# Residual two-block transformer on one core: 512-column products from a joined high and low operand, the last residual by transposes, squares on ScalarE, and SyncE outside the branch

## The chip, the cores and the metric

One Trainium2 chip, one core of it. The metric is the device time of one launch in microseconds (us). The kernel before was run three times; its median is 1277.7 us (1276.87 to 1277.78). PE is TensorE, ACT is ScalarE, DVE is VectorE, POOL is GpSimd, SP is SyncE, whose queue issues the transfers from HBM.

## The reference, cut to what matters

256 tokens of width 1024 go through two models in a row, all in float32.

- Block 1: an input projection into two attentions (8 heads each) and two gates, `mixed = sigmoid(gate_a)*(o_a@w_o_mla) + sigmoid(gate_b)*(o_b@w_o_moba)`, `x += mixed@w_out`, then a mixture of 32 experts (each token uses 2) and a final norm.
- Block 2, layer 0: `x += even_mixer(norm(x))` (a gated convolution beside differential attention). Layer 1: `x += odd_mixer(norm(x))` (stick-breaking attention, 16 heads of 64).
- In both layers of block 2 then: `x += mem_attention(norm(x), memory)` (4 heads of 256) and `x += ffn(norm(x))` with `u = causal_conv3(h@w_up)`, `gate, val = split(u)`, `(silu(gate)*val)@w_down`, where `w_up` is 1024 x 5632 and `w_down` 2816 x 1024.

All weights are read once; most of the time is their products with 256 token columns.

## The kernel before, in words

**Products.** A float32 product is made from three float32r products: the weight and the activation are each split into a high and a low part, and `h*xh + h*xl + l*xh` is summed in PSUM (`mm3`). An activation lies feature-major as `[128, 8 chunks, 256 tokens]` in two tiles, `xh` and `xl` (`xtiles`, `parts`). A weight comes in slabs of 1 MB (`slab`): SP issues the transfer into `w`, then in two halves ACT copies `w` to `h` and DVE subtracts `w - h` into `l`. `w`, `h` and `l` have three buffers each.

**fm** multiplies a slab of 8 chunks x 256 output columns: for each chunk and each of the two blocks of 128 output columns three matmuls of 256 moving columns, 48 in a slab, all into one PSUM bank (tag `g`, three banks), the two blocks side by side. The evictions read this bank with one DVE instruction, a multiplication by the row of `1/rms` (`rbc`):

```
b = self.fm(self.slab(a[f"w_up{l}"][i], 256), x)
nc.vector.tensor_tensor(u[:, :, 2:], self.two(b), self.rep(rbc), ALU.mult)
```

**Where the change touches it.** `block1_attention` makes the gates (8 slabs); `mem_attention` the queries (4 slabs in each layer, `head_norm` evicts them); `odd_mixer` queries and keys (8 slabs); `ffn` the up-projection (22 slabs in each layer, pairs of gate and value columns). After two up slabs, `ffn` does one slab of the down-projection (`down`), whose four PSUM banks (two of tag `a`, two of tag `b`) stay open for the whole stage. In layer 0, `down` makes 48 matmuls of 256 columns a slab, in layer 1 (token-major, for the output) 24 of 512. In layer 1 the residual enters these four banks first, by 16 products of `self.x` with the identity; at the end ACT and DVE in turn copy the banks to `o`, and SP stores them.

**rsq** makes `1/sqrt` by ACT (Ln, Exp) and one Newton step on DVE, whose first instruction is `u*u`. `transposed` turns a tile of probabilities with PE and copies it from PSUM with DVE.

**Order of the work.** `Recorder` records every operation, then `plan` puts them in order by a list schedule with a cost for each (a 256-column float32r matmul at 109.7 ns, a 512-column one at 216.3 ns), a lag of 200 ns between engines and a number of buffers for each tag; every engine runs its own list in that order. Transfers are issued by SP in the order of recording, each when the plan has a buffer for it. All recorded operations show as line 470.

**The branch.** After the second of eight groups of experts, `moe_late` handles tokens over an expert's 32 slots (none in this run): `values_load` reads a flag into a register of each engine (line 1210), and `tc.If(late > 0)` (line 1220) is taken by all engines, SP too, since the transfers of the branch body are SP's. `plan` lets all engines but SP stop there.

## Time and profile before

| what | value |
|---|---|
| median of 3 runs | 1277.7 us |
| the profiled execution's own time | 1279.2 us |
| its span | 1277.4 us |
| busy: PE, DVE, ACT, POOL | 1224.6, 862.5, 647.3, 7.8 us |
| granted PE clock, mean over the span | 0.977 of full |
| read from HBM | 270.96 MB |

The span is the time from the first to the last instruction in the trace. The profiled execution took 1.8 us more than its span and 1.5 us more than the median. A matmul's duration in the trace overlaps the next one's; how long a stream of matmuls takes is read from their starts, or from the chain of waits, which gives a group's time without overlap.

### The profile page before, as it was taken

The page shows a single profiled execution, that of the slowest core. Times are in us where ns is not written, and L with a number is a line of the kernel's source. Part 1 is how long each engine was busy: PE and PEld are TensorE (multiplying, and loading weights), DVE is VectorE, ACT ScalarE, POOL GpSimd, SP SyncE. Part 2 cuts the span into 40 slices and gives each one's busy share as a digit, 9 for nine tenths or more (in the row PEclk, how much of TensorE's full clock was granted, in tenths as well). Part 3 has the DMA queues.
Part 4 walks back from the last instruction along what each step waited for, and adds up shares of the span by engine and source line. Part 5 has one row for each costly group of instructions (what it writes and reads, how often), then busy time and mean ns, then how long its engine had stood idle before and what let it go on. Part 6 is the DMA issues. An engine that isn't in the chain of part 4 may idle for free.

```text
span 1277.4 us, 22372 instructions
## 1 busy us (share of the span) xinstructions
PE 1224.6 (96%) x9175; PEld 1077.6 (84%) x9175; DVE 862.5 (68%) x1546; ACT 647.3 (51%) x1095; POOL 7.8 (1%) x70
## 2 busy tenths in 40 slices
PE   9999999997889878998999999999999999999998
PEld 8988999664555644897999999999989999999997
DVE  7667677424462345997877977777755587877775
ACT  7655554223242234564545655555766655555543
POOL 0000000000000000000000000000000000000000
PEclk9999999998899989998999999999999999999999
DMA  7623565898999987532441554555433252554541
GB/s 263 245 99 133 207 253 200 335 403 359 419 412 419 416 366 296 198 132 100 162 169 65 200 195 171 195 186 178 165 133 133 93 178 98 193 193 173 184 176 66
DMA packets 40140, 273.51 MB, mean 214 GB/s; under 512 B 4576, under 2 KB 4576, under 8 KB 8032
## 3 DMA queue, kind: packets, MB, share of 16 engines
q1 hardware_dynamic: 40032, 272.03, 56.9%
q8 instruction: 73, 1.20, 0.4%
q14 instruction: 35, 0.29, 0.1%
HBM read 270.96 MB, written 1.05 MB: 213 GB/s over the span
## 4 chain that ended last, share of the span: by engine, by line
PE 90%; DVE 5%; ACT 3%; issue 1%; DMA 1%; SPq 0%; DVEq 0%; ACTq 0%
PE fm L470 51%; PE dn L470 10%; PE tm L470 6%; PE tw L470 4%; PE gu L470 4%; PE by L470 2%; PE oz L470 2%; PE bo L470 1%; DVE l L470 1%; PE sc L470 1%; PE mo L470 1%; PE ga L470 1%; PE ms L470 1%; PE co L470 1%; PE hn L470 1%; ACT h L470 1%
## 5 line engine op out<-in xcount | busy, mean ns | idle before, releaser
L470 PE MATMUL fm<-xh,h 128*128 128x256 f32 x1824 | 529.1, 291 | 7.3 <-ACT h L470 5.0
L470 PE MATMUL fm<-xh,l 128*128 128x256 f32 x1824 | 521.5, 286 | 5.8 <-DVE l L470 5.8
L470 PE MATMUL fm<-xl,h 128*128 128x256 f32 x1824 | 521.0, 286 | 0.0
L470 DVE TENSOR_TENSOR l<-w,h 128x1024 fp32r<-128x1024 f32 (+2 forms) x328 | 383.4, 1190 | 61.7 <-ACT h L470 60.4
L470 ACT ACTIVATE h<-w 128x1024 fp32r<-128x1024 f32 (+2 forms) x328 | 325.6, 1026 | 170.9 <-issue 87.7
L470 PEld LDWEIGHTS fm<-xh,h 128*128 128x128 f32 x1824 | 353.3, 194 | 18.3 <-ACT h L470 7.5
L470 PEld LDWEIGHTS fm<-xh,l 128*128 128x128 f32 x1824 | 353.2, 194 | 8.9 <-DVE l L470 8.6
L470 PEld LDWEIGHTS fm<-xl,h 128*128 128x128 f32 x1824 | 353.6, 194 | 6.5 <-issue 5.1
L470 DVE SCALAR_TENSOR_TENSOR fc<-fu,partile,fc 128x256 f32<-128x256 f32 x176 | 73.4, 478 | 1.3 <-ACT fc L470 1.3
L470 PE MATMUL gu<-w,xs 128*32 128x512 f32 x512 | 69.0, 646 | 0.2 <-PEq L1220 0.2
L470 PE MATMUL dn<-fa,h 128*128 128x256 f32 x352 | 64.2, 282 | 1.1 <-ACT fa L470 0.6
L470 PE MATMUL tm<-l,xh 128*128 128x256 f32 (+2 forms) x204 | 60.1, 296 | 2.7 <-DVE l L470 2.7
L470 PE MATMUL tm<-h,xh 128*128 128x256 f32 (+2 forms) x204 | 61.0, 300 | 0.8 <-DVE x L470 0.6
L470 PE MATMUL tm<-h,xl 128*128 128x256 f32 (+2 forms) x204 | 59.7, 294 | 0.0
L470 PE MATMUL dn<-h,fa 128*128 128x512 f32 x176 | 57.0, 396 | 0.0
L470 DVE TENSOR_TENSOR fu<-fm,rbc 128x512 f32<-128x512 f32 x44 | 30.2, 687 | 38.3 <-PE fm L470 38.0
L470 PEld LDWEIGHTS dn<-fa,h 128*128 128x128 f32 x352 | 54.4, 189 | 1.6 <-ACT fa L470 0.8
L470 DVE SCALAR_TENSOR_TENSOR yl<-by,rw,yh 128x512 fp32r<-128x512 f32 x16 | 12.0, 749 | 57.1 <-ACT yh L470 57.1
L470 PE MATMUL dn<-fa,l 128*128 128x256 f32 x176 | 49.6, 282 | 0.0
L470 ACT ACTIVATE fc<-fc 128x256 f32<-128x256 f32 x44 | 18.4, 418 | 56.3 <-DVE fc L470 56.2
L470 PEld LDWEIGHTS tm<-h,xh 128*128 128x128 f32 x204 | 39.7, 195 | 5.9 <-issue 3.1
L470 ACT ACTIVATE hn_sq<-hn_raw 128x512 f32<-128x512 f32 x20 | 12.3, 624 | 60.7 <-DVE hn_raw L470 60.7
(285 smaller groups left out, 1572.0 us busy)
## 6 DMA issues: line engine op xcount, KB each, us to landing
w<-w_gu SPq DMA_DIRECT2D x64, 1024.0 KB, 9.7
w<-w_up SPq DMA_DIRECT2D x44, 1024.0 KB, 4.9
w<-w_dn SPq DMA_DIRECT2D x32, 1024.0 KB, 11.6
w<-w_down SPq DMA_DIRECT2D x22, 1024.0 KB, 4.9
w<-w_xkv SPq DMA_DIRECT2D x16, 1024.0 KB, 7.7
w<-w_in_d SPq DMA_DIRECT2D x8, 1024.0 KB, 4.8
w<-w_xq SPq DMA_DIRECT2D x8, 1024.0 KB, 4.9
w<-w_xo SPq DMA_DIRECT2D x8, 1024.0 KB, 5.0
```

What stands on the lines that cost most here:

```text
L470: self.last[engine.engine] = getattr(engine, method)(*map(r, a), **{n: r(v) for n, v in k.items()})
```

## The change

- `xtiles` gives one tile `xx` with `xh` and `xl` behind each other (two buffers), in place of two tiles.
- `fm_wide` takes the place of `fm` in the gates (8 slabs), the queries of `mem_attention` but the first of each layer (6), the odd mixer's queries and keys (8) and the up slabs 3 to 19 of each `ffn` (34). For each block of 128 output columns it uses a bank of its own: a matmul of `h` over the 512 columns `xh | xl`, then one of `l` over the 256 columns of `xh` into the first half. ACT copies the first half out, DVE adds the second, and DVE multiplies by `rbc`.
- From block 2 on (`by_act`), the `u*u` in `rsq` is a Square on ACT. In the even mixer the copy of transposed probabilities is ACT's.
- In the last `ffn` the identity products are gone. After the sixth up slab, 16 transposes of `x` go through bank `m` (one buffer) to a tile `xt`, copied by ACT in four pieces. At the end DVE adds `xt` to each of the four banks.
- The flag is loaded by PE, ACT, DVE and POOL alone, the hints ahead of the branch go to these four, and the transfers inside the branch body are POOL's.

```diff
@@ -24,6 +24,7 @@
...
 NPAIR = 22
+NARROW = 3
 WARM = 44
@@ -168,6 +169,7 @@
...
     AHEAD = 120
+    HERE = (mybir.EngineType.PE, mybir.EngineType.Activation, mybir.EngineType.DVE, mybir.EngineType.Pool)
     FIRST = "natural_log_exp_and_others"
@@ -450,7 +452,7 @@
...
             if n in early:
-                for engine in mybir.ALL_ENGINES:
+                for engine in self.HERE:
                     if engine in self.last:
@@ -590,7 +592,8 @@
...
     def xtiles(self):
-        return [self.rec.tile([128, KC, T], F32R, n, n, 2) for n in ("xh", "xl")]
+        both = self.rec.tile([128, 2, KC, T], F32R, "xx", "xx", 2)
+        return both[:, 0], both[:, 1], both
@@ -621,7 +624,10 @@
...
         nc.scalar.activation(u, u, AF.Exp, scale=-0.5)
-        nc.vector.tensor_tensor(t, u, u, ALU.mult)
+        if self.by_act:
+            nc.scalar.activation(t, u, AF.Square)
+        else:
+            nc.vector.tensor_tensor(t, u, u, ALU.mult)
         nc.vector.scalar_tensor_tensor(t, ms, eps, t, ALU.add, ALU.mult)
@@ -689,10 +695,29 @@
...
+    def fm_wide(self, w, x, kcs=None, cols=0):
+
+
+        (h, l), _ = w
+        xh, _, both = x
+        kcs = kcs or [(k, k) for k in range(KC)]
+        bs = []
+        for j in range(2):
+            b = self.bank("g", "fw")
+            s = slice(cols + 128 * j, cols + 128 * j + 128)
+            for i, (k, c) in enumerate(kcs):
+                self.rec.record("tensor", [
+                    ("matmul", (b[:, :512].rearrange("p (a b) -> p a b", a=2), h[:, k, s], both[:, :, c, :]),
+                     dict(start=i == 0, stop=False, skip_group_check=True)),
+                    ("matmul", (b[:, :T], l[:, k, s], xh[:, c, :]),
+                     dict(start=False, stop=i == len(kcs) - 1, skip_group_check=True))])
+            bs.append(b)
+        return bs
+
     def tm(self, b, w, x, kcs, t, cols, first=True, last=True):
@@ -773,12 +798,15 @@
...
-    def transposed(self, p, e):
+    def transposed(self, p, e, by_act=False):
         b = self.bank(p, "pt")
...
         pt = self.temp(p, "pt", [128, 384])
-        self.rec.vector.tensor_copy(pt, b[:, :384])
+        if by_act:
+            self.rec.scalar.activation(pt, b[:, :384], AF.Copy)
+        else:
+            self.rec.vector.tensor_copy(pt, b[:, :384])
         return pt
@@ -929,8 +957,11 @@
...
             for s in range(4):
-                b = self.fm(self.slab(a["w_in_d"][4 * n + s], 256), x)
-                nc.vector.tensor_tensor(gates[n][:, 2 * s:2 * s + 2, :], self.two(b), self.rep(rbc), ALU.mult)
+                for j, b in enumerate(self.fm_wide(self.slab(a["w_in_d"][4 * n + s], 256), x)):
+                    gv = gates[n][:, 2 * s + j, :]
+                    nc.scalar.activation(gv, b[:, :T], AF.Copy)
+                    nc.vector.tensor_tensor(gv, gv, b[:, T:], ALU.add)
+                    nc.vector.tensor_tensor(gv, gv, rbc, ALU.mult)
         for g in gates:
@@ -1207,14 +1238,15 @@
...
         x, hh, hl, rtm, wlate, ident = (v.real() for v in (self.x, hh, hl, rtm, wlate, self.ident))
-        late = nc.values_load(flag.real()[0:1, 0:1], min_val=0, max_val=2 * T)
+
+        late = nc.values_load(flag.real()[0:1, 0:1], engines=rec.HERE, min_val=0, max_val=2 * T)
         tile = lambda shape, name, tag: rec.pools["sb"].tile(shape, F32, name=name, tag=tag, bufs=rec.bufs[tag])
...
             w = tile([128, 512], "wl", "tb")
-            nc.sync.dma_start(w, ap)
+            nc.gpsimd.dma_start(w, ap)
             return w
@@ -1314,7 +1346,13 @@
...
         raw = self.temp(p, "hn_raw", [128, 2, T])
-        nc.vector.tensor_tensor(raw, self.two(b), self.rep(rbc), ALU.mult)
+        if isinstance(b, list):
+            for j in range(2):
+                nc.scalar.activation(raw[:, j, :], b[j][:, :T], AF.Copy)
+                nc.vector.tensor_tensor(raw[:, j, :], raw[:, j, :], b[j][:, T:], ALU.add)
+            nc.vector.tensor_tensor(raw, raw, self.rep(rbc), ALU.mult)
+        else:
+            nc.vector.tensor_tensor(raw, self.two(b), self.rep(rbc), ALU.mult)
         sq = self.temp(p, "hn_sq", [128, 2, T])
@@ -1385,7 +1423,8 @@
...
             p = "ab"[s % 2]
-            b = self.fm(self.slab(a[f"w_xq{l}"][s], 256), x)
+            slab = self.slab(a[f"w_xq{l}"][s], 256)
+            b = self.fm_wide(slab, x) if s else self.fm(slab, x)
             q = self.temp(p, "mq", [128, 2, T])
@@ -1465,7 +1504,7 @@
...
                 stt(ps[0][:, s], ps[0][:, s], rs[0][:, t:t + 1], ps[1][:, s], ALU.mult, ALU.add)
-            pt = self.transposed(p, ps[0])
+            pt = self.transposed(p, ps[0], True)
             bo = self.bank(p, "bo")
@@ -1525,11 +1564,12 @@
...
             p = "ab"[i % 2]
-            b = self.fm(self.slab(a["w_oqk"][i], 256), x)
             qk = self.temp(p, "oqk", [128, 2, T])
             q, k = qk[:, 0, :], qk[:, 1, :]
-            nc.vector.tensor_tensor(q, b[:, :T], r8, ALU.mult)
-            nc.vector.tensor_tensor(k, b[:, T:], rbc, ALU.mult)
+            for qv, b, r in zip((q, k), self.fm_wide(self.slab(a["w_oqk"][i], 256), x), (r8, rbc)):
+                nc.scalar.activation(qv, b[:, :T], AF.Copy)
+                nc.vector.tensor_tensor(qv, qv, b[:, T:], ALU.add)
+                nc.vector.tensor_tensor(qv, qv, r, ALU.mult)
             if i % 4 == 0:
@@ -1567,11 +1607,7 @@
...
         acs = [self.bank("aabb"[i], f"dn{i}") for i in range(4)]
-        if out is not None:
-            for c in range(KC):
-                for t in range(2):
-                    self.mm(acs[2 * t + c // 4][:, 128 * (c % 4):128 * (c % 4) + 128],
-                            self.x[:, c, 128 * t:128 * t + 128], self.ident, c % 4 == 0, False)
+        xt = None
         fas = []
@@ -1591,15 +1627,21 @@
...
                         m = slice(512 * n, 512 * n + 512)
-                        self.mm3([(acs[2 * t + n], part(0, k, s), part(1, k, s), h[:, k, m], lo[:, k, m], False,
-                                   i == ndown - 1 and k == 1) for k in range(2)])
+                        self.mm3([(acs[2 * t + n], part(0, k, s), part(1, k, s), h[:, k, m], lo[:, k, m],
+                                   i == 0 and k == 0, i == ndown - 1 and k == 1) for k in range(2)])
...
             p = "ab"[i % 2]
-            b = self.fm(self.slab(a[f"w_up{l}"][i], 256), x)
+            slab = self.slab(a[f"w_up{l}"][i], 256)
             u = self.temp(p, "fu", [128, 2, T + 2])
             nc.gpsimd.memset(u[:, :, 0:2], 0.0)
-            nc.vector.tensor_tensor(u[:, :, 2:], self.two(b), self.rep(rbc), ALU.mult)
+            if not NARROW <= i < NPAIR - 2:
+                nc.vector.tensor_tensor(u[:, :, 2:], self.two(self.fm(slab, x)), self.rep(rbc), ALU.mult)
+            else:
+                for n, b in enumerate(self.fm_wide(slab, x)):
+                    nc.scalar.activation(u[:, n, 2:], b[:, :T], AF.Copy)
+                    nc.vector.tensor_tensor(u[:, n, 2:], u[:, n, 2:], b[:, T:], ALU.add)
+                nc.vector.tensor_tensor(u[:, :, 2:], u[:, :, 2:], self.rep(rbc), ALU.mult)
             cs = self.temp(p, "fc", [128, 2, T])
@@ -1611,6 +1653,16 @@
...
                 down(i // 2 - 1)
+            if i == 5 and out is not None:
+
+                xt = self.big("xt", [128, 2, D])
+                for t in range(2):
+                    for n in range(2):
+                        b = self.bank("m", "xt")
+                        for j in range(4):
+                            nc.tensor.transpose(b[:, 128 * j:128 * j + 128],
+                                                self.x[:, 4 * n + j, 128 * t:128 * t + 128], self.ident)
+                        nc.scalar.activation(xt[:, t, 512 * n:512 * n + 512], b, AF.Copy)
         down(ndown - 1)
@@ -1619,17 +1671,16 @@
...
                 o = self.temp("ab"[i % 2], "o", [128, 512])
-                if i % 2:
-                    nc.vector.tensor_copy(o, acs[i])
-                else:
-                    nc.scalar.activation(o, acs[i], AF.Copy)
+                nc.vector.tensor_tensor(o, acs[i], xt[:, t, 512 * n:512 * n + 512], ALU.add)
                 nc.sync.dma_start(out[128 * t:128 * t + 128, 512 * n:512 * n + 512], o)
...
     def record(self, out):
+        self.by_act = False
         steps = self.memory()
...
         x, rbc = self.two_norms()
+        self.by_act = True
         for l in range(2):
...
                 self.odd_mixer()
```

## Rows read from the trace of the kernel before

**Rows 1.** The page: busy time of the engines, and the chain's shares by engine.

```profile
PE 1224.6 (96%) x9175; PEld 1077.6 (84%) x9175; DVE 862.5 (68%) x1546; ACT 647.3 (51%) x1095; POOL 7.8 (1%) x70
...
PE 90%; DVE 5%; ACT 3%; issue 1%; DMA 1%; SPq 0%; DVEq 0%; ACTq 0%
```

**Rows 2.** Chain of waits from 895 us, last feed-forward: start, us, what.

```profile
1081.25 3.57 PE dn L470 x32
...
1113.90 11.51 PE fm L470 x96
1125.40 5.61 PE dn L470 x24
...
1262.37 11.25 PE dn L470 x48
1273.64 0.69 DVE o L470
```

**Rows 3.** Busy time by stretch, first feed-forward: PE, PEld, DVE, ACT, POOL, clock, DMA, GB/s.

```profile
700.00:720.00 20.00, 20.00 (x167) 19.95 (x167) 18.99 (x29) 14.76 (x22) 0.00 (x0) 1.00 0.70 258
...
740.00:780.00 40.00, 40.00 (x336) 40.00 (x335) 31.08 (x48) 21.48 (x33) 0.41 (x4) 1.00 0.51 181
```

**Rows 4.** Timeline of PE, 512-column matmuls of block 1: start, us of one.

```profile
55.19 0.39 PE L470 MATMUL tm<-h,xh 128*128 128x512 f32 x1
...
59.04 0.39 PE L470 MATMUL tm<-h,xl 128*128 128x512 f32 x1
```

**Rows 5.** Chain of waits, 512-column matmuls of the odd mixer.

```profile
904.94 4.80 PE tw L470 x21
909.96 4.98 PE tw L470 x21
```

**Rows 6.** Groups by form of ACT and DVE: busy us, mean ns | idle before.

```profile
L470 ACT ACTIVATE h<-w 128x1024 fp32r<-128x1024 f32 x306 | 311.0, 1050 | 163.2 <-issue 87.7 <-PE fm L470 55.9 <-PE tw L470 14.4
...
L470 ACT ACTIVATE xh<-bo 128x256 fp32r<-128x256 f32 x16 | 6.1, 382 | 10.1 <-PE bo L470 9.9
...
L470 DVE TENSOR_TENSOR l<-w,h 128x1024 fp32r<-128x1024 f32 x306 | 366.9, 1220 | 55.2 <-ACT h L470 53.8
...
L470 DVE COPY pt<-pt 128x384 f32<-128x384 f32 x20 | 10.8, 553 | 8.3 <-PE pt L470 8.1
...
L470 DVE TENSOR_TENSOR rsq_t<-rsq_u 128x256 f32<-128x256 f32 x20 | 8.3, 422 | 9.0 <-ACT rsq_u L470 8.9
...
L470 DVE TENSOR_TENSOR xl<-bo,xh 128x256 fp32r<-128x256 f32 x16 | 6.7, 419 | 8.9 <-ACT xh L470 8.8
```

**Rows 7.** Line 1220, the branch: count, durations in ns, first and last start.

```profile
L1220 SPq EVENT_SEMAPHORE  x8: 17/17/17, 300.5 to 309.1; - x8
...
L1220 SPq COMPARE_BRANCH  x1: 70/70/70, 295.3 to 295.3; - x1
```

**Rows 8.** Timeline of SP around the branch: start, us, issues.

```profile
288.11 22.31 SPq L470 DMA_DIRECT2D w<-w_gu  x4
```

**Rows 9.** Transfers, 285 to 320 us in 40 slices of 0.875 us.

```profile
GB/s 290 243 356 272 440 421 412 440 431 440 412 431 421 421 440 421 412 412 412 431 440 375 412 393 253 94 28 0 0 159 253 440 449 412 374 421 421 449 449 431
```

**Rows 10.** Busy time by stretch, the experts after the branch (columns as in rows 3).

```profile
320.00:400.00 80.00, 69.94 (x510) 44.40 (x509) 38.41 (x74) 26.29 (x41) 0.00 (x0) 0.93 1.01 416
400.00:480.00 80.00, 68.42 (x484) 42.37 (x483) 28.38 (x50) 22.56 (x31) 0.00 (x0) 0.91 0.95 391
```

**Rows 11.** Timeline of PE, transposes of x in block 1, and what follows them.

```profile
212.20 1.03 PE L470 MATMUL xt<-csttile,x 128*128 128x128 f32 x8
213.17 0.62 PE L470 MATMUL rt<-x,wr 128*36 128x256 f32 x2
```

**Rows 12.** Busy time by stretch: end of the even mixer's attention, odd mixer, queries.

```profile
580.00:600.00 20.00, 14.67 (x86) 12.50 (x86) 18.32 (x51) 10.19 (x29) 0.20 (x2) 0.77 0.30 106
960.00:1000.00 40.00, 40.00 (x328) 36.91 (x327) 21.76 (x34) 27.65 (x51) 0.00 (x0) 1.00 0.37 130
1020.00:1060.00 40.00, 40.00 (x288) 37.99 (x287) 35.42 (x69) 19.45 (x40) 0.31 (x3) 1.00 0.50 182
```

More of the change, by code (lines that the diff above doesn't have):

```diff
@@ L668, in norm_parts @@
         acc = None
-        xh, xl = self.xtiles()
+        xh, xl, both = self.xtiles()
         for i in range(4):
@@ L674, in norm_parts @@
                 acc = self.sumsq(src, [i], acc)
-        return (xh, xl), acc
+        return (xh, xl, both), acc
     def fm(self, w, x, kcs=None, cols=0, name="fm", tag="g"):
         (h, l), _ = w
-        xh, xl = x
+        xh, xl = x[:2]
         b = self.bank(tag, name)
@@ L690, in fm @@
         return b
+    def fm_wide(self, w, x, kcs=None, cols=0):
[14 more added lines that the diff above has]
+        return bs
     def tm(self, b, w, x, kcs, t, cols, first=True, last=True):
         (h, l), _ = w
-        xh, xl = x
+        xh, xl = x[:2]
         ts = slice(128 * t, 128 * t + 128)
@@ L1061, in moe @@
         nc, a, x = self.rec, self.a, self.x
-        hh, hl = (t.rearrange("p (t q) n -> p t (q n)", t=2) for t in self.xtiles())
+        hh, hl = (t.rearrange("p (t q) n -> p t (q n)", t=2) for t in self.xtiles()[:2])
         for q in range(2):
@@ L1279, in two_norms @@
         nc.vector.tensor_tensor(fg2, self.par("final_norm"), self.par("final_norm"), ALU.mult)
-        xh, xl = self.xtiles()
+        xh, xl, _ = self.xtiles()
         acc = self.tile([128, 512], "acc", "acc", 2)
@@ L1343, in prepare @@
             m = state["m"].rearrange("p (c t) -> p c t", t=T)
-            xh, xl = self.xtiles()
+            xh, xl, _ = self.xtiles()
             acc = None
```

## The prediction, made before the change was run

> **What bounds the kernel now.** The page's first part comes first: PE is busy 96% of the span, DVE 68%, ACT 51%, and the chain of work that ended last runs to 90% over PE [rows 1]. That share is an average over unlike stages, so the chain by place comes next. In the last feed-forward it is PE and nothing else: two up slabs (96 matmuls) in 11.51 us, one down slab in 5.62 us, over and over, to the last copy [rows 2]. In the first feed-forward the view by stretches has PE busy for all 40 us of 740 to 780, while DVE has 31.1 and ACT 21.5 [rows 3]. There every nanosecond off a matmul comes off the time. Two stages are different. After the branch in the experts the transfers are busy 95 to 101% of the time at about 400 GB/s, and PE is not full [rows 10]: HBM is the bound, so a hole in the transfers costs its whole length. At the end of the even mixer PE has 14.7 of 20 us and DVE 18.3 [rows 12]: DVE's chain is the bound.
>
> **The wide products.** A chunk of one output block costs three 256-column matmuls now. On the chain that is 11.51/96 = 0.1199 us each [rows 2], 0.3597 for three. [...] Afterwards the chunk is one matmul of 512 columns and one of 256. No row has these two in alternation, nor a moving operand in two pieces, so 512 columns are taken from their nearest relatives. [...] In the odd mixer the chain gives 4.80/21 = 0.2286 and, for the next group, 4.98/21 = 0.2371 [rows 5]; the down slabs give 5.62/24 = 0.2342 [rows 2]. [...] A chunk then costs 0.2286 + 0.1199 = 0.3485, saving 0.0112 us. There are 56 wide slabs (8 gates, 6 queries, 8 in the odd mixer, 34 up slabs) with 16 such chunks: 896 x 0.0112 = **10.0 us less**. The ends are 11.9 (0.2265) and 2.5 (0.2371); if the two-piece operand cost as two matmuls it would be 0, and a loss is excluded only as far as the column count stays at 768.
>
> [...]
>
> **What the eviction adds.** A wide slab adds two ACT copies of 256 columns from PSUM (382 ns each by the nearest row) and two DVE additions (419 ns) [rows 6]; the gates and the odd mixer replace a multiplication by others of about the same sum. That is 0.76 us of ACT and 0.84 us of DVE a slab, 43 and 47 us in all. In the feed-forward they lie beside PE. Per 17.1 us DVE now has 31.08 x 17.1/40 = 13.3 us and would have 15.0 of some 16.8; ACT goes from 9.2 to 10.7 [rows 3]. So they cost nothing there; without that cover they cost up to the rival below. In the queries and the odd mixer PE is full as well [rows 12], but each head's chain gets a copy and an addition longer (0.8 us) while the matmuls that cover it get shorter. I charge **1.0 us** for 14 such slabs, between 0 and 3 (0.2 us each).
>
> **SP out of the branch.** SP compares at 295.3 us and then handles eight semaphores, the last at 309.1 [rows 7]; between its issues of expert weights lie 22.3 us from 288.11 [rows 8]. The transfers show the result: seven slices of 0.875 us at 253, 94, 28, 0, 0, 159 and 253 GB/s among slices of about 420 [rows 9]. Missing are (7 x 420 - 787) x 0.875/420 = 4.5 us of transfers. Queued behind SP's wait are the next gate and up weights, two down slabs and a memory slab; PE waits for them. Without it SP can issue each as its buffer comes free. The four other engines still stop, POOL too, but POOL's list has only small memsets (7.8 us busy in all [rows 1]), and the body's transfers are not run. Since the rest of the experts runs at the transfer limit [rows 10], I count **4.0 us less**, between 0 (PE frees buffers too late to fill the hole) and 4.5.
>
> **The last residual.** The identity products take 3.57 us on the chain at 1081.25 [rows 2]. In their place come 16 transposes, 0.97 us for eight [rows 11], so 1.94: **1.6 us less**. That holds if they were not covering the wait for the norm. The start of the first feed-forward has none of them, and PE is full there, 20.0 of 20 [rows 3]; so what comes next is ready. The transposes share one bank with ACT's four copies; the plan can put other matmuls between. At the end, the last bank is read by one DVE instruction before and after (0.69 us [rows 2]): nothing. [...]
>
> **Squares and copies on ACT.** In the even mixer four copies (553 ns) and the squares (422 ns at 256 columns) leave DVE [rows 6], where DVE is the bound [rows 12]. Each is in a chain and only changes engine, so most of it is not won. I take **0.8 us less**, between 2.2 (the four copies whole) and a loss of 1. Elsewhere it lies beside PE. The joined tile `xx`, the hints and NARROW's slabs cost nothing: they add no instruction to a full engine.
>
> **The sum.** 10.0 + 4.0 + 1.6 + 0.8 - 1.0 = 15.4 us. The profiled execution (1279.2, span 1277.4) would come to 1263.8. The median of the runs shown stands 1.5 us lower, so 1277.7 - 15.4 = **1262.3 us**.
>
> **The rivals.**
>
> [...] The 512-column matmul costs 0.2371 in every wide slab. For it speaks that the same shape drifts between 0.2265 and 0.2371 within block 1 and the odd mixer [rows 4, 5] and stays at 0.2342 in the down slabs of the very stage [rows 2]; against it the steady 0.1199 of the up slabs beside them. Then 2.5 us are won in place of 10.0: 1269.8 us. Chance 12%. [...]
>
> *The hole in the transfers was free.* PE frees expert buffers no sooner, so SP waits for buffers in place of semaphores. For it speaks that PE itself has stops around the branch; against it the full transfers ahead of the hole and after it [rows 9]. Then 4.0 us fall out: 1266.3 us. It is also what happens if the branch still holds SP. Chance 12%.
>
> *Banks run out, slower than before.* A wide slab fills two `g` banks where it filled one, and each needs a copy on ACT and then an addition on DVE before PE may use it again. With three banks PE comes back to one after the other two, two times 16 matmuls or about 2 x 2.8 = 5.6 us. Copy and addition are 0.8 us; behind one half slab on ACT (1.05) and two on DVE (2.44) [rows 6] they make 4.3, still less. If DVE, then 90% busy in the feed-forwards, falls further behind, PE waits in every slab. From 15.4/56 = 0.28 us a slab on, the change loses; at 0.4 us it is 22.4 - 15.4 = 7 us slower, 1284.7 us. DVE's free fifth today [rows 3] speaks against it. Chance 7%.
>
> **How the numbers follow.** The forecast has 66%, the rivals 12, 12 and 7; 3% are left to a new order of the plan that costs some us somewhere. The forecast's own ends are 1277.7 - (11.9 + 4.5 + 2.2 + 2.2) = 1256.9 and, with the 512 columns at the down slabs' 0.2342 (5.0 us won in place of 10.0), 1267.3. The range goes from 1256.5 to 1271, which takes in the first two rivals one at a time and leaves out the third. A difference of under 0.2% (2.6 us) can't be told from none here. Forecast, first and second rival are all faster by more: 0.89. The third rival and half of the rest are slower: 0.07 with what of them ends near zero taken off, and 0.04 the same.
>
> **What would show it.** In the chain of the last feed-forward, two up slabs should be 64 matmuls in about 11.15 us where 96 took 11.51; 11.4 or more is the first rival. The transfers around the branch should stay near 420 GB/s with no empty slice, and SP should have no instruction at the branch. The group of the identity products should be gone, with 16 transposes of `x` in the last feed-forward. PE waits on DVE or ACT inside 740 to 780 would be the third rival. The prediction is wrong if the experts do not end about 4 us sooner relative to their start, or if the feed-forwards save less than 5 us together.

## The result and the profile after

The kernel after takes 1285.2 us (median of 5, 1282.65 to 1286.75) beside 1276.9 us for the kernel before (median of 5 run beside it): a ratio of 1.0067 [1.0045, 1.0089], so 0.7% **slower**. The prediction was 1262.3 us and faster. The profiled execution of after took 1286.75 us, its span is 1284.9. One execution of e9 (1501.9 us) and one of e10 (2911.2 us), far slower than the others, are left out of the ratios of the experiments below.

On the page of the profile, PE has fewer instructions than in rows 1 and less busy time, in a longer span; the share of the chain that runs over PE has fallen from 90% to 65%. Busy time of the engines, and the chain's shares:

```profile
PE 1216.0 (95%) x8263; PEld 1024.8 (80%) x8263; DVE 884.8 (69%) x1641; ACT 695.9 (54%) x1236; POOL 8.3 (1%) x70
...
PE 65%; DVE 6%; ACT 3%; issue 1%; DVEq 0%; ACTq 0%
```

So less work was done, and more time lost between. To find where, both timelines are cut at the last instruction of each stage (us from the span's start; the experts begin with the first `gu` matmul and end with the last addition of `co`; a mixer or a memory attention ends with its last addition to `x`, a feed-forward with its last addition or the last `o`):

| stage | before | after | difference |
|---|---|---|---|
| up to the first expert | 236.4 | 234.1 | -2.3 |
| experts | 273.3 | 277.0 | +3.7 |
| even mixer | 131.3 | 132.5 | +1.2 |
| memory attention, layer 0 | 64.9 | 69.6 | +4.7 |
| feed-forward, layer 0 | 192.3 | 189.1 | -3.2 |
| odd mixer | 120.0 | 118.5 | -1.5 |
| memory attention, layer 1 | 63.7 | 73.5 | +9.8 |
| feed-forward, layer 1 | 191.7 | 186.9 | -4.8 |

The feed-forwards and the odd mixer gained 9.5 us together. The two memory attentions alone lost 14.5, and the experts lost where they should have won.

**Feed-forwards: as forecast.** The chain of the last feed-forward (start, us, what) answers to rows 2. `fw` is a matmul of `fm_wide`, `fm` one of `fm`, `dn` one of the down-projection, `xt` a transpose of `x`:

```profile
1121.97 11.11 PE fw L472 x64
1133.07 5.62 PE dn L472 x24
1138.69 0.44 PE xt L472 x4
...
1241.41 11.29 PE fw L472 x64
1252.69 5.62 PE dn L472 x24
1258.31 11.51 PE fm L472 x96
1269.82 11.25 PE dn L472 x48
1281.07 0.02 issue
1281.10 0.69 DVE o L472
```

The chain of the first feed-forward has pairs of up slabs of this length:

```profile
741.45 11.10 PE fw L472 x64
```

Two up slabs are 64 matmuls in 11.11 or 11.29 us here, some 11.20 on average, and in 11.10 in the first feed-forward, where 96 took 11.51; the two slabs left narrow still take that. The identity products have gone, and transposes in fours of 0.44 to 0.57 us stand in the chain instead, 1.94 us in all for 3.57.

In the first feed-forward PE is full in the same 40 us as in rows 3, while DVE went from 31.1 to 34.4 us and ACT from 21.5 to 25.2; there the added evictions are hidden (first fence, columns as in rows 3). In the last memory attention PE is not full any more (second fence; the stage in three pieces, with the sum):

```profile
740.00:780.00 40.00, 40.00 (x266) 36.78 (x265) 34.41 (x58) 25.17 (x43) 0.46 (x5) 1.00 0.59 206
```

```profile
1020.70:1040.00 19.30, 19.30 (x124) 17.54 (x124) 16.92 (x26) 13.01 (x23) 0.00 (x0) 1.00 0.76 273
1040.00:1050.00 10.00, 6.64 (x24) 4.99 (x23) 6.80 (x18) 3.63 (x13) 0.00 (x0) 0.83 0.31 105
1050.00:1094.20 44.20, 42.05 (x285) 38.12 (x284) 27.34 (x52) 20.70 (x40) 0.55 (x6) 1.00 0.15 49
sum 73.50, PE 67.99 PEld 60.65 DVE 51.07 ACT 37.35 POOL 0.55; mean PE 22.66 PEld 20.22 DVE 17.02 ACT 12.45 POOL 0.18
```

PE is idle for 73.5 - 68.0 = 5.5 us of a stage that showed it full in rows 12. The worst 10 us, on PE's timeline (start, us, work, idle before and releaser) and on ACT's; `mq` is a head's query tile, `ms` its scores, `mp` its exponentials, `nm` the maxima that these need, `hn_raw` the evicted query slab:

```profile
1040.19 0.27 PE L472 MATMUL fw<-xx,l 128*128 128x256 f32 x1
1042.56 5.41 PE L472 MATMUL ms<-mk,mq 128*128 128x256 f32 x16 [2.09 <-DVE mq L472]
1049.23 0.47 PE L472 MATMUL fw<-xx,h 128*128 128x512 f32 x1 [1.26 <-DVE hn_raw L472]
```

```profile
1040.41 0.42 ACT L472 ACTIVATE rsq_t<-rsq_u 128x256 f32<-128x256 f32 x1
1046.69 0.47 ACT L472 ACTIVATE mp<-ms,nm 128x256 f32<-128x256 f32 x1 [5.87 <-DVE nm L472]
1047.06 0.19 ACT L472 ACTIVATION_READ_ACCUMULATOR mp<-ms,nm 128x1 f32 x1
1047.16 0.47 ACT L472 ACTIVATE mp<-ms,nm 128x256 f32<-128x256 f32 x1
1047.51 0.20 ACT L472 ACTIVATION_READ_ACCUMULATOR mp<-ms,nm 128x1 f32 x1
1047.61 0.65 ACT L472 ACTIVATE hn_raw<-fw 128x256 f32<-128x256 f32 x2
```

Read from the bottom. At 1047.61 ACT takes the copies of the second wide query slab. It stood idle for 5.87 us before, but in its list the exponentials of another head come first, and those wait for that head's scores (`ms`). So this slab's two banks stay full. By 1040.19 PE has done both slabs and half of the third, whose first bank is the last of the three; the other half (the 16 `fw` matmuls from 1049.23 on) needs one of the two. Nothing but scores is left to PE, of two heads together. It waits 2.09 us for them, and 1.26 us for the bank behind them. The scores are slow too, 5.41/16 = 0.338 us each. In the kernel before, on its chain of waits, eight stand between projections and take 0.216 each:

```profile
1040.18 1.73 PE ms L470 x8
```

The granted clock of the stretch is 0.83, with 1.00 on both sides; in pieces of 1 us it is 0.51, 0.50, 0.50 and 0.78 from 1043 to 1047, within the time of these scores, and 1.00 in the pieces before and behind.

The 1.26 us are the only wait of PE for a wide slab's bank that the whole trace shows. In layer 0, where the stage lost 4.7 us, PE's waits are for a head's queries (1.1 us) and its turned probabilities (0.9 us), in the order of the plan, which counts the three banks. How much of the loss is held banks, and how much the order that the plan makes of them, no run tells apart.

**The branch: SP is out of it, but DVE now stands.** Line 1252 of after (count, durations in ns, first and last start, and who waited), which answers to rows 7; a q behind an engine's name is its sequencer:

```profile
L1252 ACTq COMPARE_BRANCH  x1: 68/68/68, 304.8 to 304.8; - x1
...
L1252 DVEq COMPARE_BRANCH  x1: 84/84/84, 308.0 to 308.0; - x1
L1252 DVEq EVENT_SEMAPHORE  x1: 21/21/21, 313.7 to 313.7; - x1
...
  ACT L472: 8.3, 1
```

The same two DVE rows of the kernel before:

```profile
L1220 DVEq COMPARE_BRANCH  x1: 84/84/84, 310.3 to 310.3; - x1
L1220 DVEq EVENT_SEMAPHORE  x1: 21/21/21, 310.9 to 310.9; - x1
```

SP has no row any more. But DVE's branch takes 5.7 us until its next instruction instead of 0.6, and ACT waits 8.3 us for it instead of 3.2. PE stands behind both, at the transposes `at` of the next expert's activations (us in all, times, longest; before, then after):

```profile
PE at L470 <- DVE act L470: 1.6, 1, 1.6
```

```profile
PE at L472 <- DVE act L472: 7.7, 1, 7.7
```

The transfers show both changes. From 285 to 320 us (first fence; rows 9 for before) the empty slices have gone. They come back in the 35 us after that (second fence), in which SP waits for PE and DVE to free buffers; the kernel before has a mean of 419 GB/s in those 35 us, after 337:

```profile
GB/s 384 412 431 421 440 421 412 431 440 421 431 421 421 412 440 412 421 421 412 421 403 431 412 403 431 421 431 403 431 393 403 412 421 431 403 440 412 384 253 178
```

```profile
GB/s 206 412 403 272 328 431 253 28 150 403 412 393 421 449 421 431 431 75 28 75 140 393 421 412 440 431 431 412 421 19 150 384 431 421 403 431 421 449 431 421
```

### The profile page after: what moved, and what is told of

It reads as the page before. It is cut to its first block, busy times and chain, and to the rows that moved or that the text cites. A ratio compares the mean times of both kernels' runs of the same rounds, so it can differ in the third digit from the quotient of the medians.

```text
span 1284.9 us, 20760 instructions
## 1 busy us (share of the span) xinstructions
PE 1216.0 (95%) x8263; PEld 1024.8 (80%) x8263; DVE 884.8 (69%) x1641; ACT 695.9 (54%) x1236; POOL 8.3 (1%) x70
## 4 chain that ended last, share of the span: by engine, by line
PE 65%; DVE 6%; ACT 3%; issue 1%; DVEq 0%; ACTq 0%
PE fw L472 20%; PE fm L472 19%; PE dn L472 10%; PE tw L472 3%; PE gu L472 2%; PE tm L472 2%; DVE l L472 2%; PE oz L472 2%; PE by L472 1%; PE mo L472 1%; PE ms L472 1%; ACT h L472 1%; PE hn L472 1%; DVE x L472 1%; PE bo L472 1%
## 5 line engine op out<-in xcount | busy, mean ns | idle before, releaser
L472 PE MATMUL fm<-xx,h 128*128 128x256 f32 x1856 | 354.2, 291 | 11.7 <-DVE cu L472 5.4
L472 PE MATMUL fw<-xx,h 128*128 128x512 f32 x896 | 321.1, 399 | 1.3 <-DVE hn_raw L472 1.3
L472 PEld LDWEIGHTS fm<-xx,h 128*128 128x128 f32 x1856 | 295.4, 194 | 29.9 <-issue 9.1
L472 PE MATMUL fm<-xx,l 128*128 128x256 f32 x928 | 265.7, 288 | 6.2 <-DVE l L472 6.1
L472 PE MATMUL fw<-xx,l 128*128 128x256 f32 x896 | 251.1, 281 | 0.0
L472 PEld LDWEIGHTS fw<-xx,h 128*128 128x128 f32 x896 | 168.1, 188 | 38.2 <-issue 2.1
L472 PEld LDWEIGHTS fm<-xx,l 128*128 128x128 f32 x928 | 179.8, 194 | 9.0 <-DVE l L472 8.5
L472 PEld LDWEIGHTS fw<-xx,l 128*128 128x128 f32 x896 | 169.3, 189 | 0.7
L472 PE MATMUL tm<-h,xx 128*128 128x256 f32 (+2 forms) x408 | 83.1, 297 | 0.9 <-DVE x L472 0.6
L472 PEld LDWEIGHTS tm<-h,xx 128*128 128x128 f32 x408 | 67.0, 195 | 9.0 <-issue 5.8
```

Source lines behind the costliest of these rows:

```text
L472: self.last[engine.engine] = getattr(engine, method)(*map(r, a), **{n: r(v) for n, v in k.items()})
```

## The experiments

Each kernel ran beside the kernel before on the same chip, e1 to e8 on one chip and e9 to e14 on another, so across these two groups the ratios compare better than the medians. Stage times of the profiled executions, in us (the last column is the median of all runs):

| kernel | up to the experts | experts | even | memory 0 | ffn 0 | odd | memory 1 | ffn 1 | time |
|---|---|---|---|---|---|---|---|---|---|
| after | 234.1 | 277.0 | 132.5 | 69.6 | 189.1 | 118.5 | 73.5 | 186.9 | 1285.2 |
| e1 queries narrow | 233.6 | 275.3 | 133.9 | 65.6 | 188.4 | 118.5 | 64.6 | 186.9 | 1272.2 |
| e2 SP back | 233.5 | 279.5 | 132.2 | 69.6 | 188.4 | 118.5 | 73.5 | 186.9 | 1287.1 |
| e3 two banks, DVE | 234.2 | 274.3 | 132.5 | 65.5 | 188.4 | 118.5 | 66.0 | 186.9 | 1271.7 |
| e4 one bank, by ACT | 234.0 | 275.4 | 132.5 | 67.6 | 188.7 | 118.6 | 65.3 | 186.9 | 1274.9 |
| e5 e1 + gates narrow | 235.3 | 268.0 | 132.2 | 65.6 | 188.4 | 118.5 | 64.6 | 186.9 | 1267.2 |
| e6 e1 + late hint | 234.4 | 273.8 | 132.4 | 65.6 | 188.4 | 118.5 | 64.6 | 186.9 | 1272.0 |
| e7 e1 + squares on DVE | 234.9 | 276.3 | 131.5 | 64.9 | 188.9 | 118.5 | 63.7 | 187.4 | 1271.1 |
| e8 two banks, by ACT | 233.9 | 275.8 | 132.5 | 70.2 | 188.6 | 118.5 | 68.6 | 186.9 | 1280.6 |
| e9 e5 + wide, DVE | 235.2 | 269.5 | 132.2 | 65.7 | 189.3 | 118.5 | 66.6 | 186.9 | 1269.8 |
| e10 e5 + 24 | 235.1 | 277.0 | 132.3 | 65.6 | 188.4 | 118.5 | 64.6 | 186.9 | 1272.7 |
| e11 e5 + squares on DVE | 235.5 | 269.7 | 131.4 | 64.9 | 188.9 | 118.4 | 63.7 | 187.4 | 1264.6 |
| e12 e5 + SP back | 234.5 | 273.6 | 132.3 | 65.6 | 188.4 | 118.4 | 64.6 | 186.9 | 1269.0 |
| e13 e7 + 105 | 235.3 | 273.6 | 131.4 | 64.9 | 188.9 | 118.5 | 63.7 | 187.4 | 1266.9 |
| e14 e5 + 12 | 234.7 | 276.0 | 132.3 | 65.6 | 188.4 | 118.5 | 64.6 | 186.9 | 1272.3 |

From the first memory attention on, a stage that an edit does not touch repeats to within some tenths of a us. The experts do not: e1, e3, e4, e6, e7 and e8, which are alike there, lie between 273.8 and 276.3 us. Much of the spread is the clock. One stretch, from one addition of `co` to `x` to the next, takes 26.1 us at a mean granted clock of 0.80 in before, after, e2, e4, e10, e12 and e13, and 23.4 us at 0.93 in the others, with the same work. In e10 and in e5 (columns as in rows 3):

```profile
455.10:481.10 26.00, 19.86 (x122) 11.70 (x124) 12.31 (x25) 8.76 (x11) 0.00 (x0) 0.80 0.88 366
```

```profile
449.10:472.40 23.30, 17.12 (x122) 10.39 (x124) 12.27 (x25) 8.79 (x11) 0.00 (x0) 0.93 0.98 405
```

Only one execution of each kernel was profiled, so whether this goes with the kernel or with the execution is not shown. With 2.7 us taken off the former group, the experts take 272.7 to 276.8 us where DVE is late at the branch (after, e1 to e4, e6 to e8, e10, e14) and 268.0 to 270.9 where it is not (before, e5, e9, e11, e12, e13). The even mixer once took 133.9, also at a lower clock (0.96, where after has 0.97).

### The queries: e1, e3, e4, e8, e9

**e1** makes the queries narrow again:

```diff
-            b = self.fm_wide(slab, x) if s else self.fm(slab, x)
+            b = self.fm(slab, x)
```

> The changed kernel with the queries of the memory attention back on 256-column products in one bank; all else as changed. Theory (the wide queries lose the time: two banks and a longer eviction in a stage whose heads hang on a chain): the two memory attentions go from 69.6 and 73.5 us back to about 65 and 64, the time from 1285.2 to about 1271 (1269 to 1274). Rival (the squares on ACT or the joined tile lengthen these stages): they stay near 70 and 73 us, the time at 1283 or more.

Measured 1272.2 us, 0.9973 [0.9955, 0.9991]: 13.0 us under after, and the two memory attentions together are 130.2 us in place of 143.1. Of the 14.5 us lost in them, 12.9 are the queries'. What of them costs it? A wide slab differs in three ways: 512-column matmuls, two banks in place of one, and an eviction that goes through ACT before DVE ends it. **e3** keeps two banks but makes 256-column products and lets DVE evict them in one step (`fm_two` is `fm` with a bank for each block):

```diff
-                nc.scalar.activation(raw[:, j, :], b[j][:, :T], AF.Copy)
-                nc.vector.tensor_tensor(raw[:, j, :], raw[:, j, :], b[j][:, T:], ALU.add)
-            nc.vector.tensor_tensor(raw, raw, self.rep(rbc), ALU.mult)
+                nc.vector.tensor_tensor(raw[:, j, :], b[j][:, :T], rbc, ALU.mult)
...
-            b = self.fm_wide(slab, x) if s else self.fm(slab, x)
+            b = self.fm_two(slab, x) if s else self.fm(slab, x)
```

> The changed kernel with three 256-column products a chunk in the queries, but each block of 128 output columns in a bank of its own, multiplied out by DVE alone: two banks a slab, no copy by ACT, no addition. Theory A (the banks are what the queries lack): the memory attentions stay near 69 and 73 us, the time near 1284 (1281 to 1287). Theory B (the longer eviction is what delays the heads): they return to 65 and 64 us, the time to about 1271.

**e4** keeps one bank of 256-column products and adds the way through ACT (a copy, then a maximum of the copy with itself, which changes nothing):

```diff
-                nc.scalar.activation(raw[:, j, :], b[j][:, :T], AF.Copy)
-                nc.vector.tensor_tensor(raw[:, j, :], raw[:, j, :], b[j][:, T:], ALU.add)
+                nc.scalar.activation(raw[:, j, :], b[0][:, T * j:T * j + T], AF.Copy)
+                nc.vector.tensor_tensor(raw[:, j, :], raw[:, j, :], raw[:, j, :], ALU.max)
...
-            b = self.fm_wide(slab, x) if s else self.fm(slab, x)
+            b = [self.fm(slab, x)] if s else self.fm(slab, x)
```

> The changed kernel with 256-column products in one bank in the queries, evicted by two copies on ACT, two DVE instructions of 256 columns (in place of the additions) and the multiplication: the long eviction without the second bank. Theory A (banks): the memory attentions return to about 66 and 65 us, the time to about 1273. Theory B (the long eviction): they stay near 69 and 73 us, the time near 1284.

e3 came to 131.5 us in the two stages (1271.7 us, 0.9959 [0.9944, 0.9974]) and e4 to 132.9 (1274.9 us, 0.9987 [0.9971, 1.0003]), over 130.2 in e1. Neither alone is the loss; each expectation took one of them for all of it. **e8** does both, still with 256-column matmuls: e3's `fm_two`, and behind it

```diff
                 nc.scalar.activation(raw[:, j, :], b[j][:, :T], AF.Copy)
-                nc.vector.tensor_tensor(raw[:, j, :], raw[:, j, :], b[j][:, T:], ALU.add)
+                nc.vector.tensor_tensor(raw[:, j, :], raw[:, j, :], b[j][:, :T], ALU.max)
```

> The kernel after, with the queries made of 256-column matmuls into two banks a slab, and behind them the long eviction: a copy on ScalarE, a maximum with the bank in place of the sum on VectorE, the multiplication. If it is the two banks held through two engines that cost the queries their time, the two stages of memory attention stay at 69 to 70 and 72 to 74 us and the time at 1283 to 1286 us; if it is the 512-column matmuls themselves or the order that the planner gives them, they fall to 65 to 66 us each and the time to 1271 to 1273 us.

Measured 1280.6 us, 1.0043 [1.0023, 1.0064]; 70.2 and 68.6 us, together 138.8: as expected of the held banks in layer 0, between the two expectations in layer 1. With no 512-column matmul in the queries, 8.6 of the 12.9 us are there. The waits of PE in its last memory attention (us in all, times, longest):

```profile
PE mo L472 <- DVE mpt L472: 0.9, 1, 0.9
PE ms L472 <- DVE mq L472: 0.8, 1, 0.8
PE fm L472 <- ACT xx L472: 0.7, 1, 0.7
```

Two banks alone add 1.3 us, ACT alone 2.7, both 8.6: the two together cost more than their sum. In e4 the one bank is free as soon as ACT has copied it, while in e8 and in after DVE must read each bank as well before it is free, so the surplus can be that longer hold. The planner makes a new order for each of these kernels, and each number holds the edit together with its order. **e9** asks the opposite, in the better kernel e5 (below): real 512-column matmuls, evicted by DVE alone, with the query tile as scratch.

```diff
+            low = out
             for j in range(2):
-                nc.scalar.activation(raw[:, j, :], b[j][:, :T], AF.Copy)
-                nc.vector.tensor_tensor(raw[:, j, :], raw[:, j, :], b[j][:, T:], ALU.add)
-            nc.vector.tensor_tensor(raw, raw, self.rep(rbc), ALU.mult)
+                nc.vector.tensor_tensor(raw[:, j, :], b[j][:, :T], rbc, ALU.mult)
+                nc.vector.tensor_tensor(low[:, j, :], b[j][:, T:], rbc, ALU.mult)
+            nc.vector.tensor_tensor(raw, raw, low, ALU.add)
```

> The fifth experiment with the queries' 512-column matmuls again, but their eviction on VectorE alone: each half of each bank times the norm's factor, then one addition. If it is the way through ScalarE that holds the two banks too long, the two stages of memory attention stay near the narrow queries' 130.2 us together (128 to 132) and the time near the fifth experiment's 1267.2 (1265 to 1269). If the 512-column matmuls in two banks are enough by themselves, they come to 140 us or more and the time to 1277 or more.

132.3 us in the two stages, just over the 128 to 132 expected; 1269.8 us, 0.9948 [0.9931, 0.9964]. Its last memory attention, to be held against the sum of after above:

```profile
1010.40:1077.00 66.60, 65.08 (x429) 59.37 (x428) 53.22 (x101) 36.03 (x68) 0.54 (x6) 1.00 0.37 127
```

Without ACT in the eviction nearly all of the loss is gone, though the matmuls are wide; but it is still 2.1 us over e5's narrow queries. The 4.3 us between e8 and after come with the 512-column matmuls and the order that the planner gives them; which of the two was not tried. Some 1.9 of them can be the clock: the 16 scores of 5.41 us would take 3.46 at 0.216 each, and in e8 the clock of that stage is 1.00 throughout.

### The branch: e2, e5, e6, e10, e13, e14, e12

**e2** is after with SP in the branch again (`mybir.ALL_ENGINES` for the hints, no engine list at the load of the flag, the body's transfers on SP). The theory was that in after DVE's branch took longer because the transfers' queues were not drained.

> The changed kernel with SP back in the branch (flag, hints and transfers of the body as before). Theory (with the transfers kept full, DVE's own branch takes 5.7 us in place of 0.6, and PE stands 8.3 us behind it; the drained queue before let DVE through): DVE's branch is short again, the experts go from 277.0 to 273.3 us, the time from 1285.2 to about 1281.5 (1280 to 1283). Rival (SP out of the branch is a gain of 4 us that something else hides): the hole in the transfers comes on top, 1289.

1287.1 us, 1.0070 [1.0042, 1.0098], and DVE's branch took 6.7 us: the theory fell. **e5** goes another way. The wide gates give DVE four instructions a slab where it had one, so by the branch DVE's stream is 24 instructions longer; in the trace the branch is DVE's record 493 in after and 470 before, 23 further on. e5 is e1 with narrow gates:

```diff
-                for j, b in enumerate(self.fm_wide(self.slab(a["w_in_d"][4 * n + s], 256), x)):
-                    gv = gates[n][:, 2 * s + j, :]
-                    nc.scalar.activation(gv, b[:, :T], AF.Copy)
-                    nc.vector.tensor_tensor(gv, gv, b[:, T:], ALU.add)
-                    nc.vector.tensor_tensor(gv, gv, rbc, ALU.mult)
+                b = self.fm(self.slab(a["w_in_d"][4 * n + s], 256), x)
+                nc.vector.tensor_tensor(gates[n][:, 2 * s:2 * s + 2, :], self.two(b), self.rep(rbc), ALU.mult)
```

> Queries narrow as in the first experiment, and the experts' gates back to one bank of 96 matmuls a slab and one multiplication on VectorE, so that VectorE's stream ahead of the branch is as short as in the kernel before. If the length of that stream decides whether VectorE's code behind the branch is there in time, its branch takes 0.6 us instead of 5.7, the experts' stage goes from the first experiment's 275.3 to about 270 us, and the gates' own loss is 1.0 to 1.4 us: 1267 to 1269 us against the first experiment's 1272.2. If it is something else at the branch (the drained queues, the engines without SP), the branch still takes 5 us or more, and the time is 1273 to 1274 us.

1267.2 us, 0.9946 [0.9928, 0.9964]. DVE's branch in e5:

```profile
L1249 DVEq COMPARE_BRANCH  x1: 84/84/84, 307.6 to 307.6; - x1
L1249 DVEq EVENT_SEMAPHORE  x1: 21/21/21, 308.2 to 308.2; - x1
```

0.6 us again, and the experts are 7.3 us shorter than in e1, both with the shorter of the two stretches told above. **e6** moves the branch hint instead:

```diff
-    AHEAD = 120
+    AHEAD = 60
```

> The first experiment with the hint to the branch's target put 60 instead of 120 instructions ahead. [...] If the distance has no part in it, the branch stays at 5 to 6 us and the time at 1272 us.

No change: the branch takes 5.5 us, 1272.0 us, 0.9976 [0.9961, 0.9991]. **e10** separates the gates from the place of the branch. It is e5 with 24 memsets of one element at the very start of DVE's list, some 100 us ahead of the gates and 300 ahead of the branch:

```diff
+        pad = cp.tile([128, 24], F32, name="pad")
+        for i in range(24):
+            nc.vector.memset(pad[:, i:i + 1], 0.0)
```

> The fifth experiment with 24 instructions of one element at the very start of VectorE's stream (written by hand ahead of all planned work, so the order behind them is the same), which puts its branch back at the place in the stream that it had in the kernel after. If that place decides, VectorE's branch takes 5 to 6 us instead of 0.6, the experts' stage goes from 268.0 to about 275 us, and the time from 1267.2 to 1273 to 1275 us. If the gates' own work ahead of the branch decides, nothing changes but some 1 to 2 us at the start, where VectorE waits for loads anyway: 1267 to 1269 us.

They take 0.7 us in a gap, and DVE's timeline around the branch (start, us, work, idle before) has the stop back:

```profile
307.95 1.28 DVE L472 TENSOR_TENSOR x<-x,co 128x512 f32<-128x512 f32 x2 [0.72 <-PE co L472]
316.61 0.48 DVE L472 SCALAR_TENSOR_TENSOR act<-gu,rw,act 128x256 f32<-128x256 f32 x1 [7.37 <-ACT act L472]
```

The idle time is 2.20 us in before and e5, 7.29 in after. e10 takes 1272.7 us, 0.9966 [0.9950, 0.9981]: 5.5 us over e5 by the medians, 2.5 by the ratios (0.20% of 1277; their intervals overlap), for 24 instructions that compute nothing. The experts take 274.3 us beside 268.0 with the stretch of 26.1 us set equal. **e14** has 12 of them.

> The fifth experiment with 12 of the one-element instructions in place of 24, to bracket the place at which VectorE's branch becomes late. No theory says on which side 12 lies: either 0.6 us and 1267 us, or 5 to 6 us and 1272.7 us as in the tenth experiment; a time between would speak against a threshold.

```profile
L1252 DVEq COMPARE_BRANCH  x1: 84/84/84, 308.5 to 308.5; - x1
L1252 DVEq EVENT_SEMAPHORE  x1: 21/21/21, 314.3 to 314.3; - x1
```

5.7 us at the branch, 1272.3 us, 0.9971 [0.9953, 0.9989]: the edge lies within the first 12. Does a longer stream always make the branch late? **e13** takes e7 (below; the branch late, 1271.1 us, 0.9966 [0.9951, 0.9982]) and adds 105 memsets, so that the branch is DVE's record 597, 127 behind e5's 470, a distance that the author guessed:

> The seventh experiment (queries narrow, gates wide, squares on VectorE) with 105 instructions of one element at the very start of VectorE's stream. They should take about 3.1 us there, at 30 ns each by the tenth experiment, in a gap of 4.8 us. [...] If a longer stream always makes the branch late, it stays at 5 to 6 us and the time at 1271 us.

```profile
L1255 DVEq COMPARE_BRANCH  x1: 84/84/84, 309.2 to 309.2; - x1
L1255 DVEq EVENT_SEMAPHORE  x1: 21/21/21, 309.8 to 309.8; - x1
```

0.6 us. e13 takes 1266.9 us, 0.9917 [0.9898, 0.9935]: **4.2 us faster with 105 more instructions** by the medians, and the ratios' intervals do not meet. So it is the place, and not that the stream is longer. Whether short places come back every 127 records (597 - 470) the runs do not show: 597 is the only place tried behind 494.

**e12** then prices SP where DVE is not late (e5, with the edit of e2).

> The fifth experiment, in which VectorE's branch is short, with SP in the branch again as in the kernel before: this prices SP by itself. The forecast's 4.0 us gives 1271 us, with the hole in the transfers back at 296 to 302 us and no lead afterwards; if the hole was free, 1267 to 1268 us.

1269.0 us, 0.9934 [0.9912, 0.9955], beside 0.9946 [0.9928, 0.9964] for e5: the medians say 1.8 us for SP, the ratios the other sign; not resolved. By the stages to the end of the experts, with the stretch of 26.1 us set equal, it is 2.1 us, and e2 against after (1.9 us by medians, 0.4 by ratios) says no more. The transfers say why it is small. e12 from 285 to 320 us, then e5 from 320 to 355:

```profile
GB/s 356 356 431 421 431 440 421 421 421 440 421 431 421 421 421 421 403 412 431 431 384 356 150 84 56 0 19 159 309 421 412 431 421 403 412 440 421 431 431 421
```

```profile
GB/s 403 403 431 412 421 421 393 431 412 440 431 375 234 178 159 431 449 412 412 403 440 431 346 19 94 309 412 412 421 440 431 440 440 393 431 403 421 431 440 384
```

With SP in the branch the hole is there (a mean of 363 GB/s over the 35 us, so (420 - 363)/420 x 35 = 4.8 us are lost). Without it e5 has a mean of 420 there, and then the holes of the second fence (a mean of 380, where e12 has 419): 3.3 us are given back, since SP has run ahead and waits for buffers to be freed. 1.5 us remain by this count.

### Squares and copies on ACT: e7, e11

**e7** is e1 with both on DVE again:

```diff
-            pt = self.transposed(p, ps[0], True)
+            pt = self.transposed(p, ps[0])
-        self.by_act = True
+        self.by_act = False
```

> The first experiment with the squares of the norms on VectorE again and the even mixer's copies of the transposed rows too. The forecast put ScalarE's part at a gain of 0.8 us over all, so the time would be 1273 us; the rival, that a ScalarE that is asked for a further step holds up the even mixer (133.9 us in the first experiment, 131.3 in the kernel before), gives 131.5 us there and 1270 us in all.

**e11** makes the same edit in e5.

> The fifth experiment with the squares and the even mixer's copies on VectorE: a candidate for the best version. The forecast's term (ScalarE saves 0.8 us) gives 1268 us; the seventh experiment, which differed from the first by 1.0 us downwards, gives 1266 us.

e7 takes 1271.1 us, 0.9966 [0.9951, 0.9982], 1.0 us under e1, which can't be told from none by itself; e11 takes **1264.6 us, 0.9904 [0.9884, 0.9924]**, 2.7 us under e5 and the fastest of all. The two stages of memory attention are 64.9 and 63.7 us, to the tenth what they were before the change, where e1 and e5 have 65.6 and 64.6; the even mixer is 0.8 us shorter than in e5; each feed-forward is 0.5 longer. From the even mixer on that is 1.5 us in all. Which wait a square on ACT lengthens was not looked for. e11 is what is left of the change when the queries, the gates and the squares go back: wide products in the feed-forwards and the odd mixer, the last residual, SP.

## Why the prediction was wrong, point by point

- **Wide products (10.0 us less): right, where the evictions are hidden.** A chunk saves (11.51 - 11.20)/32 = 0.0097 us by the chain of the last feed-forward and (11.51 - 11.10)/32 = 0.0128 by that of the first, forecast 0.0112. The forecast had 0.3485 us a chunk; these are 11.20/32 = 0.3500 and 11.10/32 = 0.3469. Its 0.2286 for the 512-column matmul is the first chain of rows 5, and that the wide slabs would have this value, between the ends 0.2265 (the mean step of rows 4, (59.04 - 55.19)/17) and 0.2371, was the author's estimate; no run shows it in a wide slab apart from the 256-column matmul beside it. The first rival (0.2371, so 11.4 us a pair) did not come. The first feed-forward gained 3.2 us, the odd mixer 1.5 (its forecast is 8 x 16 x 0.0112 = 1.4). The gates' part (1.4 us) could not be told from none in the whole time: e1 and e10, both with a late branch, wide and narrow, lie at 1272.2 and 1272.7 us. Up to the first expert, the wide gates of after and e1 to e8 (without e5) have 233.5 to 234.9 us and the narrow ones of e5, e9 to e12 and e14 234.5 to 235.5, which leaves about 1 us for them at most (e13, wide too, has 235.3).
- **The eviction in queries and odd mixer (1.0 us more, at most 3): the step that failed.** "Each head's chain gets a copy and an addition longer (0.8 us)" was priced at 1.0/14 = 0.07 us a slab, 0.2 at most, as if only the instructions' own length counted. In the queries the cost was 12.9 us, some 2.1 a slab, and that is net of what the products save. As the trace of after shows it, the copies stand in ACT's list behind exponentials that wait for another head, and meanwhile two of three banks are held; the runs show that it takes two banks and the way through ACT together (8.6 us, where either alone costs 1.3 or 2.7). That the hold itself makes the surplus, and not the plan's new order, is argued from the trace. "PE is full as well" was taken for cover, but with the longer eviction PE is idle for 5.5 us in the last of these stages. In the odd mixer, which also evicts by ACT and then DVE, none of the charge shows (1.5 us gained, 1.4 forecast before the charge); why was not tried.
- **The third rival had the mechanism and the wrong place.** It let banks run out in the feed-forwards at 0.4 us a slab and came to 1284.7 us, beside the measured 1285.2. There PE never waited for them; its one wait for a wide slab's bank is 1.26 us, in the queries, 6 of the 56 slabs. The agreement of the number is chance.
- **SP out of the branch (4.0 us less): over-sized.** The hole of 4.5 us did go. The second rival (PE frees buffers no sooner) was nearer: some 1.5 to 2.1 us remain, within what can be told from none. Of the two signs of being wrong that the prediction named, this one came: the experts end 3.7 us later relative to their start, not about 4 sooner. The other, feed-forwards that save less than 5 us, did not (8.0).
- **A term was missing.** "The four other engines still stop" took their stops as they were. DVE's grew by 5.1 us, because the gates' 24 instructions shift the branch. It cost 2.5 to 5.5 us (e10 against e5, ratios and medians), as much as SP's gain or more. The gates' extra instructions were counted as DVE time, not as places in a stream.
- **Last residual (1.6 us less): about right.** The last feed-forward gained 4.8 us and the first, with the same wide slabs, 3.2. The difference is 1.6, and so is 3.57 - 1.94 on the chains. The end of 2.2 us that the forecast's range has for it is shown by no run. It was not run by itself.
- **Squares and copies on ACT (0.8 us less): the wrong sign.** Taking them back gains 1.0 and 2.7 us by the medians, 0.9 and 5.4 by the ratios, 1.5 by the stages of e11 against e5.

The miss is 1285.2 - 1262.3 = 22.9 us. For the queries the sum had 6 x 16 x 0.0112 = 1.1 us won and 6/14 of 1.0 lost, 0.7 less in all, where 12.9 more were measured: 13.6. The branch is 2.5 to 5.5, SP 4.0 - 1.5 = 2.5, the squares 1.8 to 3.5. Together that is 20.4 to 25.1.

## What to carry to other kernels

A longer eviction is priced where its first instruction stands in its engine's list: ask what that instruction queues behind, for whom that waits, and how many banks stay full meanwhile. An edit ahead of a branch that adds instructions moves the branch, and what each engine does after the branch is to be read engine by engine, before a stage that looks slower is blamed on its work. A resource freed early (SP) is worth only what the next limit behind it leaves.

## What the runs showed of the hardware that was not expected

DVE's way past the branch, whose body is skipped in every run, took 0.6 us or 5.5 to 6.7 us, and the place of the branch in DVE's stream decided: record 470 (before, e5) short, 482 (e14), 493 (after) and 494 (e10) long, 597 (e13) short. A move of the hint's distance changed nothing (5.5 us in e6). The trace has two queues of the kind "instruction", one with packets of 16384 bytes and one with packets of 8192 (in before 73 packets, 1.20 MB, and 35 packets, 0.29 MB). Whether they have to do with the 5 us no run shows, and the records do not name the engine that a packet was for. Nor do the runs settle a period: that 470 and 597, 127 apart, are both short is one pair. So why DVE passes in 0.6 us at some places and not at others stays open.
